# Reordering the start of a gated-MLP kernel: half-column products ahead of two turns, 16-bit turns, and one late product

## The chip, the cores and the metric

The kernel runs on one core of one Trainium2 chip. The metric is the device time of one execution in microseconds (us). Several executions are made of each kernel. "TensorE" is the matmul engine (PE in profile lines, PEld its weight loads), "VectorE" is DVE, "ScalarE" is ACT, "GpSimd" is POOL, "SyncE" is SP.

## The reference

```python
batch, seq, dim, hidden = 16, 256, 512, 2048
def reference(x, w1, w2):              # x (16,256,512), w1 (512,4096), w2 (2048,512), all float32
    h = x @ w1
    gate, value = np.split(h, 2, axis=-1)
    h = np.maximum(gate, 0) * value
    return (h @ w2).astype(np.float32)
```

## The kernel before

The 4096 rows of x are done in four groups of 1024, each as two halves of 512 rows. The hidden size is cut into 16 blocks of 128. Both matrix products use a seven-product scheme: instead of eight block products there are seven (P1 to P7), and some operands are sums. On the x side these are S1 to S4, made by VectorE in the first group; on the weight side T1 to T4, made by GpSimd:

```python
    def sums_of(o, eng=nc.vector):                       # S1 = A21+A22, S2 = S1-A11, S4 = A12-S2, S3 = A11-A21
        for n, i0, i1, op in (("S1", "A21", "A22", ADD), ("S2", "S1", "A11", SUB), ("S4", "A12", "S2", SUB),
                              ("S3", "A11", "A21", SUB)):
            yield eng.tensor_tensor(o[n], o[i0], o[i1], op=op)
# ... cut
    def w1_ops(jb, n, t):
        # ... cut
        nc.gpsimd.tensor_tensor(op["T1"], b12, b11, op=SUB)
        nc.gpsimd.tensor_tensor(op["T2"], b22, (op["T1"]), op=SUB)
        nc.gpsimd.tensor_tensor(op["T3"], b22, b12, op=SUB)
        nc.gpsimd.tensor_tensor(op["T4"], b21, (op["T2"]), op=SUB)
# ... cut
    WX = {"P1": ("B11", "A11"), "P2": ("B21", "A12"), "P3": ("B22", "S4"), "P4": ("T4", "A22"),
          "P5": ("T1", "S1"), "P6": ("T2", "S2"), "P7": ("T3", "S3")}
```

Block 2 is the first in this scheme. It needs S1 and T1 for P5, S2 and T2 for P6, S4 for P3, S3 and T3 for P7. Blocks 0 and 1 are "plain" (ordinary products), so that TensorE has work while the first sums and differences are made. The very first x rows come as float32 and are turned (transposed) by TensorE, four row blocks a half; each turn is evicted from PSUM by VectorE (one part) and then ScalarE (the other part). Fillers (`keep_busy`) are matmuls without a use.

```python
    def turn_first(o, h, b, ps):
        for e in range(4):
            nc.tensor.transpose(ps[:, e * P:(e + 1) * P], xn[h][b][:, e * P:(e + 1) * P], ident)
        for k, copy in ((0, nc.vector.tensor_copy), (1, nc.scalar.copy)):
            copy(out=o[f"A{h + 1}{k + 1}"][:, :, b * P:(b + 1) * P],
                 in_=ps[:, k * 256:k * 256 + 256].rearrange("p (b t) -> p b t", b=2))
# ... cut
    turn_first(xo, 0, 0, new_w())
    keep_busy(2)
    turn_first(xo, 0, 1, new_x())
    rest()
    keep_busy(4)
    turn_first(xo, 0, 2, new_x())
    keep_busy(2)
    turn_first(xo, 0, 3, new_w())
    keep_busy(2)
    plain[0].products(0, *first_half, half)
    # ... cut: weights of block 1, a fetch
    plain[0].products(0, *first_half, other)
    plain[0].value()                                     # ScalarE copies the value product
    plain[0].gate(0)                                     # VectorE: max(gate, 0) * value
    plain[1].products(0, *first_half, half)
    ps = [new_x(), new_w()]
    for b in range(4):
        turn_first(xo, 1, b, ps[b % 2])
        if b == 1:
            plain[1].products(0, *first_half, other)
            plain[1].value()
    plain[1].gate(0)
    sums = sums_of(xo)
    prepare(2)                                           # T1 to T4 of blocks 2 and 3
    copy_some(3)
    fetch(5, nc.sync)
    next(sums)                                           # S1
    plain[0].products(1, *second_half, half)
    next(sums)                                           # S2
    next(sums)                                           # S4
    plain[0].products(1, *second_half, other)
    plain[0].value()
    plain[0].gate(1)
    prepare(3)
    plain[1].products(1, *second_half)
```

In the lines of the profile, `x_A` is one of A11, A12, A22, and `x_S` one of S1 to S4 (A21 shares the place of S3), `w_T` one of T1 to T4.

## Time and profile before

| | before |
|---|---|
| device time, first measurement | 311.19 us median of 3 (311.07 to 311.42) |
| span of the profiled run | 309.2 us |
| TensorE busy | 301.5 us, 98% |
| TensorE idle after 23.73 us, until its last products | none shown |
| P4 of block 2 (the last stalled matmul) | 23.30 us |
| S1 on VectorE, T1 on GpSimd dispatched | 15.12 us, 15.57 us |

The page of the profile of the kernel before, part 1 (busy time, share of the span, number of instructions):

```profile
PE 301.5 (98%) x1870; PEld 183.2 (59%) x1870; DVE 236.4 (76%) x378; ACT 177.0 (57%) x350; POOL 153.7 (50%) x186
```

TensorE is the limit nearly everywhere. So a change at the start can win only by letting its unbroken run begin earlier. The timeline of the kernel before shows how that moment is set (columns: start in us, duration in us, engine, line, operation, output<-input, shapes, count, and in brackets the engine's idle time before it and what ended it):

```profile
15.12 0.68 DVE L164 TENSOR_TENSOR x_S<-x_S,x_A 128x1024 f16<-128x1024 f16 x1
15.57 1.36 POOL L215 TENSOR_TENSOR w_T<-w_stage 128x512 f16<-128x512 f32 x1 [5.44 <-DMA w_stage<-in_w_dram]
15.84 1.64 DVE L164 TENSOR_TENSOR x_S<-x_S,x_A 128x1024 f16<-128x1024 f16 x1
17.01 1.49 POOL L216 TENSOR_TENSOR w_T<-w_stage,w_T 128x512 f16<-128x512 f32 x1
17.51 1.53 DVE L164 TENSOR_TENSOR x_S<-x_A,x_S 128x1024 f16<-128x1024 f16 x1
18.45 1.72 POOL L217 TENSOR_TENSOR w_T<-w_stage 128x512 f16<-128x512 f32 x1
...
19.56 1.16 DVE L164 TENSOR_TENSOR x_S<-x_A,x_S 128x1024 f16<-128x1024 f16 x1
20.13 1.61 POOL L218 TENSOR_TENSOR w_T<-w_stage,w_T 128x512 f16<-128x512 f32 x1
...
23.30 0.59 PE L233 MATMUL Y<-x_A,w_T 128*128 128x512 f16 x2 [0.47 <-DVE cc L266]
```

The four VectorE lines are S1, S2, S4 and S3; the four GpSimd lines T1 to T4. All sums have the same shape, yet S1 takes 0.68 us and S2 1.64: S2 is dispatched at 15.84, when T1 is under way, and ends at 17.48, 0.55 us after T1's end (16.93), which is near the 0.68 us of an undisturbed sum. The Trainium skill (SBUF — State Buffer, "Who interferes with whom") says that a VectorE instruction with two SBUF inputs contends with a GpSimd instruction that reads SBUF, and that whoever issues first gets the shared ports for the whole instruction. The durations here fit that. From S1 to the `cc` that releases P4 at 23.30, VectorE has no recorded wait for another engine's result: its own instructions, held up by T1 to T4, set the moment.

The list of what TensorE waited for in the kernel before, from 5 us on (engine, what, line, waited for; total us, times, longest us):

```profile
PE X L448 <- DMA x_A<-in_x_dram: 0.8, 1, 0.8
PE Y L233 <- DVE cc L266: 0.5, 1, 0.5
PE X L233 <- ACT Y L240: 0.2, 1, 0.2
```

### The profile page before, as it was taken

To read this page: it belongs to the slowest core of one execution; us is meant where nothing else is said; L and a number is where in the kernel's file an instruction comes from. 1 tells how busy PE (TensorE), PEld (TensorE's weight loads), DVE (VectorE), ACT (ScalarE), POOL (GpSimd) and SP (SyncE) were. 2 spreads that over 40 slices of the span, in tenths; PEclk is the share of its full clock that TensorE was granted. 3 is DMA by queue.
4 is the path that set the end of the run, shared out by engine and by line. 5 is a ranking of instruction groups with operands and counts; after the bars stand their busy time and mean duration, and the time that the engine had idled before them with its cause. 6 is when DMAs were issued, how large, how long until landed. Compare 5 with 4: busy or idle time off the path is not lost.

```text
span 309.2 us, 5211 instructions
## 1 busy us (share of the span) xinstructions
PE 301.5 (98%) x1870; PEld 183.2 (59%) x1870; DVE 236.4 (76%) x378; ACT 177.0 (57%) x350; POOL 153.7 (50%) x186
## 2 busy tenths in 40 slices
PE   7999999999999999999999999999999999999994
PEld 3844444588854444478864444458884444448883
DVE  1598888889678888887538888888536888888841
ACT  2588886445865555537855555546956555553231
POOL 2199999930048899500028889700006988700000
PEclk9999999999999999999999999999999999999999
DMA  7977696998594233001354400000325110000132
GB/s 236 355 230 251 176 232 87 196 214 149 164 303 101 69 70 68 2 0 47 127 184 105 119 0 4 0 0 15 122 103 171 37 34 1 0 3 0 70 136 72
DMA packets 37340, 32.87 MB, mean 106 GB/s; under 512 B 14400, under 2 KB 32320, under 8 KB 37184
## 3 DMA queue, kind: packets, MB, share of 16 engines
q1 hardware_dynamic: 31904, 25.70, 27.2%
q0 software_dynamic: 4352, 6.29, 11.8%
q10 hardware_dynamic: 1056, 0.52, 0.6%
q8 instruction: 15, 0.25, 0.3%
q14 instruction: 13, 0.11, 0.1%
HBM read 27.26 MB, written 12.58 MB: 129 GB/s over the span
## 4 chain that ended last, share of the span: by engine, by line
PE 93%; DVE 2%; DMA 2%; issue 1%; SPq 0%; ACT 0%; DVEq 0%
PE Y L233 26%; PE X L233 17%; PE W L233 17%; PE Y L333 14%; PE X L333 9%; PE W L333 9%; DMA x_A<-in_x_dram 2%; DVE x_S L164 1%; PE X L448 1%; DVE g L308 1%; PE X L301 1%; PE W L301 1%; PE W L448 0%; PE Y L150 0%; DVE x_S L450 0%
## 5 line engine op out<-in xcount | busy, mean ns | idle before, releaser
L233 PEld LDWEIGHTS <-w_T 128*128 128x128 f16 x496 | 48.5, 98 | 57.5 <-issue 1.0
L170 POOL TENSOR_TENSOR fold<-xh 128x1024 f32<-128x1024 f16 x16 | 30.3, 1894 | 93.1 <-DMA xh<-x 92.1
L233 PE MATMUL X<-x_A,w_B 128*128 128x512 f16 x248 | 73.7, 379 | 0.2 <-ACT Y L240 0.2
L233 PE MATMUL Y<-x_S,w_T 128*128 128x512 f16 x248 | 73.8, 379 | 0.0
L233 PEld LDWEIGHTS <-w_B 128*128 128x128 f16 x372 | 36.4, 98 | 42.6 <-issue 0.8
L240 ACT COPY Y<-X 128x512 f32<-128x512 f32 x62 | 35.4, 570 | 39.8 <-PE X L233 39.5
L260 DVE SCALAR_TENSOR_TENSOR cc<-W,pu 128x512 f32<-128x512 f32 x62 | 42.8, 691 | 19.5 <-ACT pu L254 19.5
L254 ACT ACTIVATE pu<-Y 128x512 f32<-128x512 f32 x62 | 37.0, 597 | 34.1 <-PE Y L233 32.8
L173 POOL TENSOR_TENSOR fold<-fold 128x512 f32<-128x512 f32 (+2 forms) x96 | 51.8, 540 | 7.5
L333 PEld LDWEIGHTS <-w_stage 128*128 128x128 f16 x512 | 50.0, 98 | 6.3 <-issue 0.4
L266 DVE SCALAR_TENSOR_TENSOR cc<-Y,pu 128x512 f32<-128x512 f32 x62 | 42.8, 691 | 7.2 <-PE Y L233 0.7
L261 DVE SCALAR_TENSOR_TENSOR g<-X,cc 128x512 f16<-128x512 f32 x62 | 42.9, 691 | 2.3
L276 DVE SCALAR_TENSOR_TENSOR g<-Y,cc 128x512 f16<-128x512 f32 x62 | 42.2, 681 | 1.8 <-PE Y L233 1.8
L333 PEld LDWEIGHTS <-g 128*128 128x128 f16 x384 | 37.6, 98 | 8.2
L233 PE MATMUL Y<-x_A,w_T 128*128 128x512 f16 x124 | 36.9, 379 | 0.5 <-DVE cc L266 0.5
L247 ACT ACTIVATE pu<-W 128x512 f32<-128x512 f32 x62 | 37.2, 600 | 0.2 <-ACT Y L240 0.2
L233 PE MATMUL W<-x_S,w_T 128*128 128x512 f16 x124 | 36.9, 379 | 0.0
L233 PE MATMUL W<-x_S,w_B 128*128 128x512 f16 x124 | 36.9, 379 | 0.0
L333 PE MATMUL Y<-v_T,w_stage 128*128 128x256 f16 x256 | 33.2, 272 | 0.1
L333 PE MATMUL X<-v_B,g 128*128 128x256 f16 x256 | 31.9, 273 | 0.0
L164 DVE TENSOR_TENSOR w_stage<-g 128x1024 f16<-128x1024 f16 x32 | 21.5, 686 | 0.2
L365 DVE SCALAR_TENSOR_TENSOR o<-W,pu 128x256 f32<-128x256 f32 x16 | 6.7, 422 | 18.7 <-PE W L333 18.7
(84 smaller groups left out, 283.8 us busy)
## 6 DMA issues: line engine op xcount, KB each, us to landing
out_dram<-o SPq DMA_DIRECT2D x30, 256.0 KB, 2.0
w_stage<-in_w_dram SPq DMA_DIRECT2D x14, 512.0 KB, 5.7
x<-in_x_dram POOLq DMA_DIRECT2D x4, 1024.0 KB, 12.9
xh<-x SPq DMA_DIRECT2D x16, 256.0 KB, 3.1
v_B<-in_w_dram POOLq DMA_DIRECT2D x3, 512.0 KB, 6.3
x_S<-in_x_dram SPq DMA_DIRECT2D x4, 256.0 KB, 5.5
x_A<-in_x_dram SPq DMA_DIRECT2D x3, 256.0 KB, 4.9
w_stage<-in_w_dram ACTq DMA_DIRECT2D x2, 256.0 KB, 4.6
```

What stands on the lines that cost most here:

```text
L164: yield eng.tensor_tensor(o[n], o[i0], o[i1], op=op)
L170: nc.gpsimd.tensor_tensor(fold, t, t, op=MULT)
L173: nc.gpsimd.tensor_tensor(fold[:, :, :m], fold[:, :, :m], fold[:, :, m:2 * m], op=ADD)
L233: nc.tensor.matmul(ps, wop[wn][:, b, self.jb * P:(self.jb + 1) * P], self.xo[xn][:, b, :], start=fresh and b == 0, stop=b == 1, skip_group ...
L240: nc.scalar.copy(out=self.Y, in_=self.X)
L247: nc.scalar.activation(self.p5, self.W, COPY, scale=GS)
L254: nc.scalar.activation(self.u2, self.Y, COPY, scale=GS)
L260: nc.vector.scalar_tensor_tensor(out=self.c12, in0=self.W, scalar=GS, in1=self.u2, op0=MULT, op1=ADD)
L261: nc.vector.scalar_tensor_tensor(out=self.g[:, self.jb, :TH], in0=self.X, scalar=0.0, in1=self.c12, op0=MAX, op1=MULT)
L266: nc.vector.scalar_tensor_tensor(out=self.c22, in0=self.Y, scalar=GS, in1=self.p5, op0=MULT, op1=ADD)
L276: nc.vector.scalar_tensor_tensor(out=self.g[:, self.jb, TH:], in0=self.Y, scalar=0.0, in1=self.c22, op0=MAX, op1=MULT)
L333: nc.tensor.matmul(ps, self.op[an][:, i], vop[wn][:, i], start=name in ("P1", "P5") and i == 0, stop=i == NJ // 2 - 1, skip_group_check=True)
```

## The change

The intent was to take idle and useless time out of TensorE's start. (a) The products of block 0 on the first half of the columns run as soon as two turns are evicted, ahead of turns three and four; most fillers go. (b) The second half of the first x is cast to 16 bit before it is turned (two casts on VectorE, two on GpSimd), so that turns and evictions are shorter. (c) The last plain value product runs after P1 of block 2, to cover TensorE's 0.23 us wait for ScalarE's copy of P1. PSUM banks are handed out differently to allow it. The diff, cut:

```diff
-        def products(self, h, a1, a2, cols=(0, TH)):
+        def open(self, W=None): ...
+        def part(self, which, a1, a2, cols=(0, TH)): ...        # gate or value products alone
 # ... cut
+    x16_first = [halfs.tile(...) ... for _ in range(2)]
+    ident16 = wpool.tile([P, P], F16, name="ident16")
+    def cast_first(b, copy):
+        copy(out=x16_first[b // 2][:, b % 2], in_=xn[1][b])
-    def turn_first(o, h, b, ps):
+    def turn_first(o, h, b, *ps):
+        rows, one = (x16_first[b // 2][:, b % 2], ident16) if h else (xn[0][b], ident)
 # ... cut
-    turn_first(xo, 0, 0, new_w())
-    keep_busy(2)
-    turn_first(xo, 0, 1, new_x())
+    spare, turns2 = new_y(), new_y()
+    turn_first(xo, 0, 0, spare, turns2)
+    keep_busy(4)
+    turn_first(xo, 0, 1, new_x(), new_x())
     rest()
-    keep_busy(4)
-    turn_first(xo, 0, 2, new_x())
-    keep_busy(2)
-    turn_first(xo, 0, 3, new_w())
-    keep_busy(2)
-    plain[0].products(0, *first_half, half)
+    nc.tensor.matmul(spare, warm_b[:, :P], warm_b[:, :TH], start=True, stop=True)
+    plain[0].open()
+    plain[0].part("gate", *first_half, half)
+    plain[0].part("value", *first_half, half)
+    turns = new_x()
+    turn_first(xo, 0, 2, turns)
+    turn_first(xo, 0, 3, turns2)
 # ... cut
     plain[0].value()
+    cast_first(0, nc.vector.tensor_copy)
+    cast_first(1, nc.gpsimd.tensor_copy)
     plain[0].gate(0)
+    plain[1].open()
+    plain[1].part("gate", *first_half)
+    turns, turns2_16 = turns.bitcast(F16), turns2.bitcast(F16)
+    turn_first(xo, 1, 0, turns)
+    plain[1].part("value", *first_half, half)
+    turn_first(xo, 1, 1, turns2_16)
+    plain[1].part("value", *first_half, other)
+    plain[1].value()
+    cast_first(2, nc.gpsimd.tensor_copy)
+    cast_first(3, nc.vector.tensor_copy)
+    turn_first(xo, 1, 2, turns)
     plain[1].gate(0)
+    plain[0].open()
+    plain[0].part("gate", *second_half, half)
+    turn_first(xo, 1, 3, turns2_16)
 # ... cut: the rest of the plain products, the sums as before
+    def last_plain():                                    # called behind P1 of block 2
+        plain[1].part("value", *second_half)
+        plain[1].value()
+        next(sums)
+        plain[1].gate(1)
```

More of the change, by code (lines that the diff above doesn't have):

```diff
@@ L142, in fast_way @@
     ident = wpool.tile([P, P], F32, name="ident")
+    Y = psy.tile([P, TH], F32, name="Y", tag="Y")
     for i in range(NWARM):
-        Y = psy.tile([P, TH], F32, name="Y", tag="Y")
         nc.tensor.matmul(Y, warm_b[:, :P], warm_b[:, :TH], start=True, stop=True)
@@ L290, in __init__, with open, part @@
             self.g, self.jb = g, jb
-        def products(self, h, a1, a2, cols=(0, TH)):
+        def open(self, W=None):
+            self.X = psx.tile([P, TH], F32, name="X", tag="X")
+            self.W = psw.tile([P, TH], F32, name="W", tag="W") if W is None else W
+        def part(self, which, a1, a2, cols=(0, TH)):
             js, c = slice(self.jb * P, (self.jb + 1) * P), slice(*cols)
-            if cols[0] == 0:
-                self.X = psx.tile([P, TH], F32, name="X", tag="X")
-                self.W = psw.tile([P, TH], F32, name="W", tag="W")
-            for a, gate, value in ((a1, "B11", "T3"), (a2, "B21", "B22")):
-                for ps, wn in ((self.X, gate), (self.W, value)):
-                    for b in range(2):
-                        nc.tensor.matmul(ps[:, c], wop[wn][:, b, js], a[:, b, c], start=a is a1 and b == 0,
-                                         stop=a is a2 and b == 1)
+            ps, names = (self.X, ("B11", "B21")) if which == "gate" else (self.W, ("T3", "B22"))
+            for a, wn in zip((a1, a2), names):
+                for b in range(2):
+                    nc.tensor.matmul(ps[:, c], wop[wn][:, b, js], a[:, b, c], start=a is a1 and b == 0,
+                                     stop=a is a2 and b == 1)
         def value(self):
@@ L440, in fast_way @@
     xn = [[t.rearrange("p a b -> p (a b)").bitcast(F32) for t in place[4 * h:4 * h + 4]] for h in range(2)]
+    x16_first = [halfs.tile([P, 8, P], F16, name="xh", tag="xh").rearrange("p (b q) c -> p b (q c)", b=2) for _ in range(2)]
+    ident16 = wpool.tile([P, P], F16, name="ident16")
     def fetch_first(h):
@@ L444, in fetch_first, with new_y @@
             nc.sync.dma_start(out=xn[h][b], in_=x_nat[0, h, b])
-    def turn_first(o, h, b, ps):
+    def cast_first(b, copy):
+        copy(out=x16_first[b // 2][:, b % 2], in_=xn[1][b])
+    def turn_first(o, h, b, *ps):
+        rows, one = (x16_first[b // 2][:, b % 2], ident16) if h else (xn[0][b], ident)
+        if len(ps) == 1:
+            ps = ps[0][:, :2 * P], ps[0][:, 2 * P:]
         for e in range(4):
-            nc.tensor.transpose(ps[:, e * P:(e + 1) * P], xn[h][b][:, e * P:(e + 1) * P], ident)
+            nc.tensor.transpose(ps[e // 2][:, e % 2 * P:(e % 2 + 1) * P], rows[:, e * P:(e + 1) * P], one)
         for k, copy in ((0, nc.vector.tensor_copy), (1, nc.scalar.copy)):
             copy(out=o[f"A{h + 1}{k + 1}"][:, :, b * P:(b + 1) * P],
-                 in_=ps[:, k * 256:k * 256 + 256].rearrange("p (b t) -> p b t", b=2))
+                 in_=ps[k][:, :2 * P].rearrange("p (b t) -> p b t", b=2))
     def new_x():
         return psx.tile([P, TH], F32, name="X", tag="X")
-    def new_w():
-        return psw.tile([P, TH], F32, name="W", tag="W")
+    def new_y():
+        return psy.tile([P, TH], F32, name="Y", tag="Y")
     fetch(0, nc.scalar)
@@ L465, in fast_way @@
     fetch(3, nc.sync)
+    nc.vector.tensor_copy(out=ident16, in_=ident)
     xo = x_tiles()
@@ L470, in fast_way @@
     rest = plain_w(0)
-    turn_first(xo, 0, 0, new_w())
-    keep_busy(2)
-    turn_first(xo, 0, 1, new_x())
+    spare, turns2 = new_y(), new_y()
+    turn_first(xo, 0, 0, spare, turns2)
+    keep_busy(4)
+    turn_first(xo, 0, 1, new_x(), new_x())
     rest()
-    keep_busy(4)
-    turn_first(xo, 0, 2, new_x())
-    keep_busy(2)
-    turn_first(xo, 0, 3, new_w())
-    keep_busy(2)
-    plain[0].products(0, *first_half, half)
+    nc.tensor.matmul(spare, warm_b[:, :P], warm_b[:, :TH], start=True, stop=True)
[5 more added lines that the diff above has]
+    turn_first(xo, 0, 3, turns2)
     plain_w(1)()
     fetch(4, nc.sync)
-    plain[0].products(0, *first_half, other)
+    plain[0].part("gate", *first_half, other)
+    plain[0].part("value", *first_half, other)
     plain[0].value()
+    cast_first(0, nc.vector.tensor_copy)
+    cast_first(1, nc.gpsimd.tensor_copy)
     plain[0].gate(0)
-    plain[1].products(0, *first_half, half)
-    ps = [new_x(), new_w()]
-    for b in range(4):
-        turn_first(xo, 1, b, ps[b % 2])
-        if b == 1:
-            plain[1].products(0, *first_half, other)
-            plain[1].value()
-    plain[1].gate(0)
+    plain[1].open()
[9 more added lines that the diff above has]
+    turn_first(xo, 1, 2, turns)
+    plain[1].gate(0)
+    plain[0].open()
+    plain[0].part("gate", *second_half, half)
+    turn_first(xo, 1, 3, turns2_16)
+    plain[0].part("value", *second_half, half)
+    plain[1].open(turns2)
+    plain[1].part("gate", *second_half, half)
     sums = sums_of(xo)
@@ L498, in fast_way @@
     next(sums)
-    plain[0].products(1, *second_half, half)
     next(sums)
+    plain[0].part("gate", *second_half, other)
+    plain[0].part("value", *second_half, other)
+    plain[0].value()
     next(sums)
-    plain[0].products(1, *second_half, other)
-    plain[0].value()
     plain[0].gate(1)
     prepare(3)
-    plain[1].products(1, *second_half)
+    plain[1].part("gate", *second_half, other)
+    def last_plain():
[3 more added lines that the diff above has]
+        plain[1].gate(1)
     LOOKX, looks = {}, []
@@ L595, in fast_way @@
                 if s == 0 and (n, jb) == ("P1", NPLAIN):
-                    plain[1].value()
-                if s == 0 and (n, jb) == ("P5", NPLAIN):
-                    next(sums)
-                    plain[1].gate(1)
+                    last_plain()
                 if n in ("P6", "P7"):
```

## The prediction

> **What bounds it now.** The list of busy times has TensorE at 98% of 309.2 us, and the chain of waits is 93% TensorE. The timeline of TensorE shows no idle time from 23.73 us to the end, so the change can only move the moment at which that unbroken run begins. Before it, TensorE waits 0.78 us for x rows (6.24 us), 0.23 for ScalarE's Y copy (18.64) and 0.47 for VectorE's `cc` of block 2 (23.30), and runs eight filler matmuls after 6.24 us (0.11 us each, 0.87 us).
>
> **Removed.** The eight fillers become one 512-column filler (0.22 us): 0.65 us less TensorE. The four later turns take 0.43 us each as 32 bit. The Trainium skill (TensorE: Matmul & The Clock Gate, Back-to-back issue gap) gives about 81 ns for a 128-column pair; no run here shows it yet. I estimate 0.32 us a turn, 0.4 less in all. Moving the last value product (0.86 us) behind P1 of block 2 hides the 0.23 us wait. At most 1.3 us of TensorE time.
>
> **Added.** Four casts of 128x512 (two on VectorE, about 0.4 us each; two on GpSimd, about 0.7 us each, from its 0.40 us for 256 elements). New waits: turns three and four now follow the half-column products, so their evictions (VectorE 0.42, then ScalarE 0.37, one after the other on a bank) end at about 9.95 us, not 9.49, and TensorE waits about 0.9 us for them. The first block's first half ends at 10.64 us (10.42 before).
>
> **What decides.** VectorE runs without a gap from 15.12 us (the first sum S1) to the end of the `cc` that releases TensorE at 23.30. There the sums alternate with GpSimd's T1 to T4: S1 alone takes 0.68 us, S2 takes 1.64, S4 1.53, S3 1.16; S2 ends after T1 ends. The Trainium skill (SBUF — State Buffer, Who interferes with whom) says that a VectorE instruction with two SBUF inputs and a GpSimd one that reads SBUF exclude each other for the whole instruction; those durations agree. T1 starts at 15.57 us, when its weights land: transfers run at about 350 GB/s from 3 us, unchanged. So what counts is when S1 starts, and that is after the last turn's ScalarE eviction.
>
> After the change: value copy of block 0 ends 11.44; gate to 12.15; evictions of turns (second half) 1 and 2 to 13.4 on ScalarE; value copy of block 1 to 14.0; gate to 14.7; last eviction 14.95 on VectorE, 15.3 on ScalarE. S1 then starts at about 15.35, 0.2 us later than before but ahead of T1. With 16-bit evictions still at 0.42 us it would come near 15.6, behind T1, and every sum would fall behind one T: about 2 us lost. If it starts by 14.8, S1 and S2 both pass ahead of T1, and about 0.75 us is won. T4 (ends at 21.74) allows at most 1.5 us.
>
> **Prediction.** Most of TensorE's gain turns into waits: 311.0 us, 8 times in 10 between 309.9 and 312.4. Faster by over 2%: 0.01; within 2%: 0.97; slower by over 2%: 0.02.
>
> **What would show it.** Later turns at 0.25 to 0.35 us; their VectorE evictions at 0.29; TensorE idle before the products after turn four; start of S1 between 14.8 and 15.5, T1 still at about 15.5; P4 of block 2 still released by VectorE's `cc`, between 22.5 and 23.7 us (23.30 before); no idle TensorE afterwards, so the times differ by that matmul's shift.
>
> **What would make it wrong.** S1 behind T1 (about 313). Or S1 early enough that T4 or TensorE sets P4 (about 310). Or later weights limiting a TensorE that runs ahead.

## The result and the profile after

| | before | after |
|---|---|---|
| device time, median (4 runs each) | 311.31 us (311.07 to 311.74) | 311.86 us (311.23 to 312.18) |
| ratio | | 1.0014, 95% interval 0.9994 to 1.0034 |
| span of the profiled run | 309.2 us | 310.4 us |
| S1, T1 dispatched | 15.12, 15.57 us | 15.42, 15.34 us |
| P4 of block 2 | 23.30 us | 24.54 us |
| last group of eight matmuls (one line of the timeline) starts | 303.50 us | 304.75 us |

A ratio is the mean time of one kernel's runs over that of the other's of the same rounds, so it is not quite the ratio of the medians quoted. By the ratio the two kernels are the same; the profiled run of the changed kernel was its slowest, and its P4 is 1.24 us late. From P4 of block 2 to the last group TensorE takes 280.20 us before (303.50 minus 23.30) and 280.21 after: the whole difference of these two profiled runs lies before P4.

Page of the changed kernel, part 1:

```profile
PE 302.0 (97%) x1865; PEld 182.5 (59%) x1865; DVE 238.2 (77%) x381; ACT 176.7 (57%) x350; POOL 155.3 (50%) x188
```

Timeline of the changed kernel, the lines that answer to those of before:

```profile
14.10 0.69 DVE L310 SCALAR_TENSOR_TENSOR g<-X,v 128x512 f16<-128x512 f32 x1 [0.21 <-ACT v L307]
14.71 0.28 DVE L462 COPY x_S<-Y 128x256 f16<-128x256 f16 x1
15.02 0.37 ACT L462 COPY x_A<-Y 128x256 f16<-128x256 f16 x1 [0.69 <-DVE x_S L462]
15.34 1.28 POOL L215 TENSOR_TENSOR w_T<-w_stage 128x512 f16<-128x512 f32 x1 [3.16 <-DMA w_stage<-in_w_dram]
15.42 1.74 DVE L164 TENSOR_TENSOR x_S<-x_S,x_A 128x1024 f16<-128x1024 f16 x1 [0.44 <-ACT x_A L462]
...
17.20 1.53 DVE L164 TENSOR_TENSOR x_S<-x_S,x_A 128x1024 f16<-128x1024 f16 x1
...
18.76 1.64 DVE L164 TENSOR_TENSOR x_S<-x_A,x_S 128x1024 f16<-128x1024 f16 x1
...
20.46 0.60 PE L233 MATMUL W<-x_S,w_B 128*128 128x512 f16 x2 [1.09 <-DVE x_S L164]
...
24.54 0.59 PE L233 MATMUL Y<-x_A,w_T 128*128 128x512 f16 x2 [0.54 <-DVE cc L266]
```

Now T1 is dispatched first, by 0.08 us. S1 takes 1.74 us instead of 0.68, and every later sum falls behind one more T. P3 of block 2 needs S4 and waits 1.09 us for it (the line at 20.46); P4 follows at 24.54. The lines above S1 show why S1 is late: the gate of block 1 (14.10) stands ahead of the last eviction on VectorE (14.71), ScalarE's part of that eviction comes behind it (15.02), and S1 waits for that.

The chain of waits of the changed kernel, from the eviction of turn four on (start, us, what; 12.87 is the eviction of the second half's second turn). Left out are TensorE's pieces from 9.87 to 12.61 us and the pieces called `issue`, of 0.05 us at most:

```profile
9.39 0.44 DVE x_A L462
12.61 0.24 PE Y L460 x4
12.87 0.30 DVE x_S L462
13.19 0.37 ACT x_A L462
13.56 0.51 ACT v L307
14.10 0.69 DVE g L310
14.79 0.21 DVE x_S L462
15.02 0.38 ACT x_A L462
15.42 1.75 DVE x_S L164
```

From 12.87 us it goes through VectorE and ScalarE alone. Ahead of that, from 9.87 to 12.85, it is TensorE's work one after the other, behind the eviction of turn four and so behind the wait for it. TensorE's new order thus helps to set the moment of S1; what it saves counts only as far as it moves that moment. The list of TensorE's waits in the changed kernel, from 5 us on:

```profile
PE W L233 <- DVE x_S L164: 1.1, 1, 1.1
PE X L302 <- DVE x_A L462: 0.6, 1, 0.6
PE Y L233 <- DVE cc L266: 0.5, 1, 0.5
```

The wait for ScalarE's Y copy (0.2) went, as intended. The wait for x rows (0.8) went from the list only because four fillers now stand in it: turn two starts at 6.23 us, against 6.24 before. A wait of 0.6 us for the evictions of turns three and four and one of 1.1 us for S4 came.

### The profile page after: what moved, and what is told of

Read it like the earlier page. It is cut to its first block, busy times and chain, and to the rows that moved or that the text cites. A ratio compares the mean times of both kernels' runs of the same rounds, so it can differ in the third digit from the quotient of the medians.

```text
span 310.4 us, 5203 instructions
## 1 busy us (share of the span) xinstructions
PE 302.0 (97%) x1865; PEld 182.5 (59%) x1865; DVE 238.2 (77%) x381; ACT 176.7 (57%) x350; POOL 155.3 (50%) x188
## 4 chain that ended last, share of the span: by engine, by line
PE 94%; DVE 4%; ACT 1%; issue 1%; DVEq 0%
PE Y L233 25%; PE X L233 17%; PE W L233 17%; PE Y L335 14%; PE X L335 9%; PE W L335 9%; DVE x_S L164 2%; PE Y L145 1%; PE X L302 1%; DVE g L310 1%; PE Y L460 0%; PE W L302 0%; DVE x_A L462 0%; PE X L460 0%; PE Y L150 0%
```

## The experiments

Two theories were put against each other. **Port order:** the time is set by whether S1 or T1 is dispatched first, and so by when S1's inputs are ready. **TensorE order:** the time is set by what TensorE does in the new order, chiefly its wait after turn four. They do not exclude each other in full, since the chain above shows TensorE's order among the things that set S1's moment; what the runs can decide is whether that order counts apart from S1's moment. All twelve runs had five rounds beside the kernel before; that kernel's own runs in these groups spread from 310.9 to 312.8 us (one at 314.3, in the group of the last four runs of the table, where it lowers all four ratios), so differences of a few tenths are read from the profiles, at P4 of block 2, more safely than from the medians. The table collects all of them (us):

| run | S1 | T1 | P4, block 2 | last group | median | ratio to before (95%) |
|---|---|---|---|---|---|---|
| before | 15.12 | 15.57 | 23.30 | 303.50 | 311.31 | |
| after | 15.42 | 15.34 | 24.54 | 304.75 | 311.86 | 1.0014 (0.9994 to 1.0034) |
| a_again | 15.25 | 15.43 | 23.44 | 304.08 | 312.07 | 1.0012 (0.9993 to 1.0030) |
| gate_late | 15.04 | 15.50 | 23.24 | 303.57 | 311.61 | 1.0000 (0.9981 to 1.0019) |
| b_delay | 15.52 | 15.51 | 24.70 | 304.92 | 312.42 | 1.0021 (1.0001 to 1.0041) |
| t_write (wrong result) | 15.25 | none | 22.08 | 302.30 | 310.01 | 0.9954 (0.9935 to 0.9972) |
| b_16 | 14.17 | 15.34 | 22.02 | 302.96 | 310.89 | 0.9988 (0.9975 to 1.0001) |
| b_last | 14.93 | 15.38 | 23.12 | 303.58 | 311.37 | 1.0001 (0.9988 to 1.0014) |
| half_only | 16.33 | 15.50 | 24.69 | 304.90 | 312.60 | 1.0041 (1.0028 to 1.0054) |
| best (wrong result) | 14.26 | 15.40 | 22.05 | 303.09 | 311.06 | 0.9989 (0.9977 to 1.0002) |
| b_16_cast | 14.30 | 15.46 | 22.16 | 302.51 | 310.51 | 0.9968 (0.9935 to 1.0002) |
| b_16_last_cast | 14.32 | 15.49 | 22.06 | 303.17 | 311.02 | 0.9987 (0.9953 to 1.0021) |
| best2 | 14.35 | 15.55 | 22.15 | 303.62 | 310.99 | 0.9977 (0.9945 to 1.0009) |
| b_cast | 14.95 | 15.38 | 23.12 | 303.33 | 311.26 | 0.9987 (0.9952 to 1.0021) |

### a_again: the changed kernel once more

No edit. Expected:

> The changed kernel itself, again. Port-order theory (VectorE's first sum S1 and GpSimd's first weight difference T1 of block 2 race for the shared SBUF port; whichever starts first holds it): the runs spread over 0.5 us or more, from about 311.2 (S1 first) to about 312.3 (T1 first); a profile with S1 at over 1.5 us has P3 of block 2 waiting about 1.1 us for S4 and P4 at about 24.5 us, one with S1 at 0.68 us has no such wait and P4 at about 23.5. TensorE-order rival (the 0.59 us wait after turn four and what follows on TensorE set the time): runs agree within 0.3 us, whatever S1 takes.

The five runs took 311.79 to 312.34 us, so the medians agree with the first measurement. The spread of 0.55 us is what was expected, but it decides nothing: the eleven runs of the kernel before in the same group spread over 1.93 us. In the profile of this run (a timeline, like those above) S1 is first:

```profile
15.25 0.69 DVE L164 TENSOR_TENSOR x_S<-x_S,x_A 128x1024 f16<-128x1024 f16 x1 [0.44 <-ACT x_A L462]
15.43 1.64 POOL L215 TENSOR_TENSOR w_T<-w_stage 128x512 f16<-128x512 f32 x1 [3.17 <-DMA w_stage<-in_w_dram]
...
23.44 0.59 PE L233 MATMUL Y<-x_A,w_T 128*128 128x512 f16 x2 [0.54 <-DVE cc L266]
...
85.90 0.60 PE L335 MATMUL Y<-v_T,g 128*128 128x256 f16 x4 [0.26 <-DVE o L372]
```

The same program: S1 takes 0.69 us and T1 1.64 (it is now T1 that waits), and P4 comes at 23.44 us, 1.10 us earlier than in the first profile. So the order at the port is not fixed in the changed kernel, and it is worth 1.1 us there. S1's 0.17 us come from far ahead: the eviction of turn three is already 0.18 us earlier (8.70 against 8.88 us). But my expectation that such a run takes 311.2 us failed: this one took 312.07. It lost 0.42 us later, and the last line shows where: a wait near 86 us that the first two profiles don't have (the brackets show 0.26 us of it, the rest is hidden in the modelled end of the matmul before). That second limit comes up again below.

### gate_late: the gate of block 1 behind S1

```diff
     turn_first(xo, 1, 2, turns)
-    plain[1].gate(0)
+    early = Plain(g, 1)
+    early.X, early.v = plain[1].X, plain[1].v
 # ... cut
     next(sums)
+    early.gate(0)
     next(sums)
```

> The changed kernel with the gate of block 1's first half moved on VectorE from before the last turn's eviction to behind S1. Port-order theory: S1 starts at about 14.95 us instead of 15.42, takes 0.68 us, T1 waits for it; the 1.1 us wait of P3 of block 2 is gone, P4 at 23.2 to 23.5 us, 311.0 +- 0.3 us, and the runs agree within 0.4 us. TensorE-order rival: TensorE's work and order are the same and its wait after turn four too, so 311.9 +- 0.3.

S1 came at 15.04, 0.46 us ahead of T1, and P3's wait was gone; P4 came at 23.24, as the port-order theory said. TensorE's wait of 0.59 us after turn four was still there, so that wait, though it lies ahead of S1, does not by itself lose the race. The median of 311.61 us misses the expected 311.0 +- 0.3 and the runs spread over 0.91 us (311.11 to 312.02), more than expected: the median alone does not tell the theories apart, the profile does.

### b_delay: S1 held back in the kernel before

```diff
+    nc.vector.tensor_copy(out=late, in_=ps[1][:, :late.shape[1]])    # 128x384 from PSUM
     sums = sums_of(xo)
     prepare(2)
```

> The kernel before with one VectorE copy of 128x384 from PSUM (about 0.5 us) put ahead of S1; nothing else touched. Port-order theory: S1 is then dispatched at about 15.65 us, behind T1 at 15.57, takes about 1.6 us, P3 of block 2 waits 0.6 us or more for S4, and the kernel loses 1.0 to 1.6 us (312.2 to 312.8): more than the 0.5 us that the copy takes. TensorE-order rival, or a plain VectorE chain without the port: it loses 0 to 0.5 us.

Timeline of b_delay:

```profile
15.06 0.55 DVE L495 CAST late<-W 128x384 f16<-128x384 f32 x1
...
15.51 1.28 POOL L216 TENSOR_TENSOR w_T<-w_stage 128x512 f16<-128x512 f32 x1 [5.44 <-DMA w_stage<-in_w_dram]
15.52 1.80 DVE L165 TENSOR_TENSOR x_S<-x_S,x_A 128x1024 f16<-128x1024 f16 x1
...
20.62 0.61 PE L234 MATMUL W<-x_S,w_B 128*128 128x512 f16 x2 [1.02 <-DVE x_S L165]
...
24.70 0.59 PE L234 MATMUL Y<-x_A,w_T 128*128 128x512 f16 x2 [0.54 <-DVE cc L267]
```

A copy of 0.55 us, with nothing of the change in it, makes the picture of the changed kernel: S1 takes 1.80 us, P3 waits 1.02 us for S4, P4 is 1.40 us late. The loss is more than twice the copy. In the times it is 1.0021, with an interval that just excludes no change.

### t_write: T1 to T4 that read nothing

For blocks 2 and 3 only, GpSimd waits for the same weights (two one-column copies) and then fills T1 to T4 with ones.

```diff
+        if jb == 2:
+            nc.gpsimd.tensor_copy(out=late[:, :1], in_=b12[:, 0, :1])
+            nc.gpsimd.tensor_copy(out=late[:, :1], in_=b22[:, 0, :1])
+            for name in ("T1", "T2", "T3", "T4"):
+                nc.gpsimd.memset(op[name], 1.0)
+        else: ...                                        # T1 to T4 as before
```

> The changed kernel with T1 to T4 of blocks 2 and 3 replaced by GpSimd memsets that start when the same weights have landed (wrong result on purpose: these weights are 1). Port-order theory: a memset reads no SBUF, so S1, S2, S4 and S3 take 0.68 us each, P3 and P4 of block 2 wait for nothing much, P4 starts at about 22.3 us and the kernel takes about 310.0 us. TensorE-order rival: S1 may shorten, but the time stays above 311.3. If T1 to T4's own durations were the limit (not the port), the sums would still take over 1 us each here.

VectorE's timeline in t_write, the four sums:

```profile
15.25 1.42 DVE L165 TENSOR_TENSOR x_S<-x_S,x_A 128x1024 f16<-128x1024 f16 x2 [0.44 <-ACT x_A L469]
16.70 0.69 DVE L165 TENSOR_TENSOR x_S<-x_A,x_S 128x1024 f16<-128x1024 f16 x1
...
17.91 0.68 DVE L165 TENSOR_TENSOR x_S<-x_A,x_S 128x1024 f16<-128x1024 f16 x1
```

The four memsets (1.92 us together, from 16.65 us) lie over S4, which takes 0.69 us all the same. So it is not GpSimd's being busy that stretches a sum, but its reading SBUF. P4 came at 22.08 us without a wait and the kernel took 310.01 us, as expected to the tenth. This run also has T2 to T4 ready earlier, so its P4 is not a measure of the port alone; the durations of the sums are.

### b_16, b_last, half_only: the three parts, each alone

b_16 puts the casts and 16-bit turns into the kernel before, in the old order (third and fourth casts ahead of turn three, on GpSimd and VectorE):

```diff
+    cast_first(0, nc.vector.tensor_copy)
+    cast_first(1, nc.gpsimd.tensor_copy)
     plain[0].gate(0)
     plain[1].products(0, *first_half, half)
-    ps = [new_x(), new_w()]
+    ps = [new_x().bitcast(F16), new_w().bitcast(F16)]
```

> The kernel before with the 16-bit turns of the second half alone (casts as in the change; order of products and turns, and the last value product, as before). Port-order theory: the first block's value copy stays at about 10.6 us, the later evictions are shorter, so S1 starts at about 14.4 us and S1 and S2 are both done or under way before T1; P4 of block 2 at about 22.3 us instead of 23.30, and the kernel is 0.7 to 1.2 us faster than before (310.2 to 310.6). Rival (16-bit turns bring the loss, by their casts and the waits on them): slower than before, S1 after 15.1.

VectorE's timeline in b_16, S1 and S2 in one line, then S4:

```profile
14.17 1.41 DVE L164 TENSOR_TENSOR x_S<-x_S,x_A 128x1024 f16<-128x1024 f16 x2
15.61 1.64 DVE L164 TENSOR_TENSOR x_S<-x_A,x_S 128x1024 f16<-128x1024 f16 x1
```

S1 and S2 take 1.41 us together, both ahead of T1 (15.34), and P4 comes at 22.02 us, 1.28 us earlier than before, without a wait for VectorE; its chain of waits is TensorE's own work but for one ScalarE copy (0.58 us) from 11.54 us on. The 16-bit turns are the helpful part. But the median is only 310.89 us: 0.4 us below its neighbours of before (311.30), and the interval just reaches 1. The lead was 1.27 us at 63 us and 0.54 us at 93 us; it was given back between, with a wait of 0.28 us near 85 us like the one in a_again.

b_last moves the last value product alone:

```diff
-    plain[1].products(1, *second_half)
+    plain[1].products(1, *second_half, only="gate")
+    def last_plain():                                    # called behind P1 of block 2
+        plain[1].products(1, *second_half, only="value")
+        plain[1].value()
+        next(sums)
+        plain[1].gate(1)
```

> The kernel before with the last plain value product moved behind P1 of block 2 alone. Port-order theory: the 0.23 us wait for ScalarE's Y copy goes, S1 and T1 stay at 15.1 and 15.5, P4 of block 2 is still set by VectorE at 23.2 to 23.4 us: no change of the time (within 0.2 us). Rival (TensorE's own time counts): 0.2 us or more faster.

The wait for the Y copy went; P4 stayed with VectorE. It came at 23.12 us, but S1 and T1 were 0.19 us early in this run as well (14.93 and 15.38), which is all of the 0.18. Time unchanged (1.0001), but that is no clean test: TensorE lost about 0.26 us near 85 us in this profile (a start-to-start of 0.70 us where 0.43 is usual), so the 0.18 us would not have shown. P4 shows it better: where VectorE sets P4, the wait ahead of it cost nothing.

half_only has the half-column products ahead of turns three and four, with the changed PSUM banks, but float32 turns and the last product in its old place:

```diff
-        rows, one = (x16_first[b // 2][:, b % 2], ident16) if h else (xn[0][b], ident)
+        rows, one = xn[h][b], ident
 # ... cut: no casts; plain[1].part("value", *second_half) and its value and gate in the old places
```

> The changed kernel without the 16-bit turns and with the last value product in its old place: the half-column products ahead of turns three and four alone (with the PSUM buffers that come with it). Port-order theory: the first value copy comes 0.5 us late as in the changed kernel, the later turns are no shorter, S1 starts at 15.6 us or later, behind T1; P4 of block 2 at 24.5 us or later; 1.0 to 1.6 us slower than before (312.2 to 312.8). Rival (the half-column move is the helpful part, the harm is in the 16-bit turns): not slower than before.

S1's inputs were ready at 16.33 us, behind T1 at 15.50. P4 came at 24.69 us, and this was the only kernel whose loss is clear of noise by a good margin: 1.0041 (1.0028 to 1.0054), all five runs between 312.49 and 312.91 us. The new order is the harmful part. The run does not split it further: the half-column products, the banks and the new places of the turns and the gate came together. Its chain of waits runs through TensorE from the wait after turn four to the third turn of the second half (14.35 us), and on through VectorE and ScalarE to S1: here TensorE's new order does set S1's moment.

### best: the evictions ahead of the gate

Here the changed kernel's last two turns go earlier and into other PSUM banks, the fourth cast goes to GpSimd, ScalarE's value copy and VectorE's gate of block 1 go behind the evictions, and the gate behind S2.

```diff
     turn_first(xo, 1, 1, turns2_16)
+    cast_first(2, nc.gpsimd.tensor_copy)
+    cast_first(3, nc.gpsimd.tensor_copy)
+    turn_first(xo, 1, 2, spare.bitcast(F16))
     plain[1].part("value", *first_half, other)
+    turn_first(xo, 1, 3, new_y().bitcast(F16))
     plain[1].value()
 # ... cut: the old places of the casts and turns, and the gate behind S2
```

> The changed kernel with all evictions of the second half ahead of block 1's value copy and gate, the fourth cast on GpSimd, the last two turns in free PSUM banks and earlier on TensorE, and the gate behind S2. Port-order theory: S1 at about 14.3 us, S2 at about 15.0, both ahead of T1 and 0.7 us each; P4 of block 2 at about 22.1 to 22.5 us; about 310.2 us, 1 us faster than before. Rival: if TensorE's earlier waits decided, these are as in the changed kernel (0.59 us after turn four), so 311.5 or more.

The result was wrong (relative error 0.21), which was not intended. A 16-bit turn fills the first 1 KB of a bank, as a matmul that starts its own sum; later block 2's Y is put into such a bank by ScalarE and added to by matmuls without a start flag. The Trainium skill (PSUM — Partial Sum Buffer, "The four PSUM rules") says that a start flag clears the accumulate bits of the whole 2 KB bank, and that a matmul without it overwrites where the bit is clear. That fits: with the turns moved to banks that a full-width matmul with a start flag fills first (best2 below), the result is right. The work and the waits are those of a right kernel, so its profile is used: S1 at 14.26, S1 and S2 in 1.42 us together, P4 at 22.05 us as expected, with TensorE's 0.59 us wait after turn four still there. The median, 311.06 us, missed the expected 310.2, by a give-back of the same kind as in b_16: its lead fell from 1.23 us at 63 us to 0.41 at 93 us.

### b_16_cast, b_16_last_cast, best2, b_cast: the second limit

In b_16, VectorE's timeline near 83 us has this line, the first two sums of the next x group:

```profile
82.65 1.42 DVE L164 TENSOR_TENSOR x_S<-x_S,x_A 128x1024 f16<-128x1024 f16 x2 [2.98 <-DMA x_A<-x]
```

VectorE waits 2.98 us there for the turned loads of the next x, and evictions of the second product queue behind it. The theory was that the three casts of x, issued together by GpSimd, slow one another down. All four runs move the cast of the third group:

```diff
-    CASTS = {(0, 11): 1, (0, 13): 0, (0, 14): 2, (1, 8): 3}
+    CASTS = {(0, 11): 1, (0, 13): 0, (0, 15): 2, (1, 8): 3}
```

b_16_cast is b_16 with it, b_16_last_cast has the last product too, best2 is the mended best, b_cast is the kernel before.

> The 16-bit turns alone on the kernel before, and the cast of the third x group moved on GpSimd from block 14 of the first group to block 15, behind the two long weight differences of the second product. Theory of the second limit (the gain of 1.27 us is given back to 0.54 between 75 and 90 us because VectorE waits there for the next x group's turned loads, whose cast shares the transfer engines with the other two casts): the next x lands 1 us or more earlier (before 81.7 us instead of 82.65), the 0.28 us wait of TensorE near 85 us is gone, the lead of P4 of block 2 (22.0 us) is kept to the end, span 307.9 to 308.1 and about 309.8 us. Rival (the late loss is VectorE's own work): unchanged at 310.9.

> The same with the last plain value product behind P1 of block 2 too. Now that VectorE no longer sets P4, TensorE's 0.23 us wait for the Y copy is on the path: P4 of block 2 at 21.7 to 21.9 us (GpSimd's T4 ends at about 21.1), about 309.6 us. Rival: T2 or the sums hold it at 22.0, same as without.

> The reordered changed kernel again, mended (the last two 16-bit turns go to banks that a matmul with a start flag fills before they are added to, so the result is right), with the cast moved as well: S1 at 14.3 us, P4 of block 2 at 22.0 us as in the wrong one, the lead kept past 85 us, about 309.9 us.

> The kernel before with only the cast moved: a control. TensorE there does not wait near 85 us, so no change: 311.2 +- 0.3 us, P4 of block 2 at 23.2 to 23.4 us; the next x lands earlier (before 82 us) all the same.

The cast theory fell. The casts did get shorter (median from issue to landing 11.3 us in b_16_cast, 14.6 in b_16), but the first sum of the next x came at 82.20, 82.85, 83.30 and 82.88 us in the four runs, not before 81.7 or 82. Only b_16_cast kept most of its lead (1.14 us at 63 us, 0.99 at 93); b_16_last_cast fell from 1.24 to 0.34 and best2 from 1.15 to 0.11 behind before. Taking the last product into b_16 moved P4 from 22.16 to 22.06, less than the 21.7 to 21.9 expected. b_cast shows no change of the time, as a control should.

TensorE's longest late wait in best2, from its timeline:

```profile
85.44 0.60 PE L335 MATMUL Y<-v_T,g 128*128 128x256 f16 x4 [0.80 <-DVE o L372]
```

One relation holds over all runs that waited there. Add 220.3 us to the moment at which VectorE's first sum of the next x starts, and the last group's start comes out: 82.65 gives 302.95 (b_16, measured 302.96), 82.20 gives 302.50 (302.51), 82.85 gives 303.15 (303.17), 83.30 gives 303.60 (303.62), 82.78 gives 303.08 (best, 303.09), 83.76 gives 304.06 (a_again, 304.08). Two more runs lie on it, with losses too short for the list of waits: 83.25 gives 303.55 (gate_late, 303.57), 83.28 gives 303.58 (b_last, 303.58). The constant is fitted to these runs. So the landing of the next x is a second floor. It varied from 82.20 to 83.76 us in these runs, hardly following the lead (82.20 to 83.30 in the five kernels that lead by over 1 us), and it caps what an earlier start can win. In the kernel before it is close already: 83.03 us there gives 303.33, only 0.17 us under the measured 303.50. So without an earlier landing hardly any of a lead at P4 could have been kept. In t_write it was no floor: there GpSimd issued the casts about 3 us earlier (51.4 us against 54.5), and VectorE's sum started at 80.86 without a recorded wait for a load. That makes an earlier issue of the casts the obvious next thing to try; no run tried it alone. What those loads wait for between their first issue at 64 us and 82 us stays open.

## Why the prediction was right, and where it was not

The measured 311.86 us lies in the range of 309.9 to 312.4, and "within 2%" was right, which says little: the median of every kernel run here, the failed ones too, lies within 0.5% of the kernel before. That the range held is partly luck: the first profile is of a run that lost to T1, which the prediction put at about 313, outside its range, and only because losing cost less than the 2 us assumed did it stay inside. Point by point:

- **The path.** That only the start of TensorE's unbroken run counts, that VectorE's chain from S1 to `cc` sets it, and that S1's moment against T1's decides, was right: a_again, gate_late and b_delay show it. That the start alone counts was not always so: a_again, b_16, b_last, best, b_16_last_cast and best2 lost time again near 85 us.
- **S1's moment.** Predicted 15.35 us; measured 15.42 and 15.25. The steps to it fit as well: 16-bit evictions on VectorE 0.28 us (0.29 predicted), the gate of block 1 ended at 14.79 (14.7), the last ScalarE eviction to 15.39 and 15.21 (15.3).
- **T1's moment, the term that was mis-sized.** The prediction took T1 as fixed at the 15.57 us of the one profile of before and concluded that S1 is "ahead of T1". In the 12 other profiles with a T1 it came at 15.34 to 15.55 us. With S1 at 15.25 to 15.42 that is a tie, not a lead of 0.2 us. The case "S1 behind T1", which the prediction named as what would make it wrong, is the one in the first profile.
- **The size of losing.** Predicted about 2 us; measured 1.24 us (after), 1.40 (b_delay) and 1.39 (half_only) against P4 of before; in the same program, lost against won, 1.10.
- **The central value.** 311.0 us is 0.2 below the time before, though the prediction's own sum put S1 0.2 us later with S1 ahead. That sum was right for a_again (P4 0.14 us later than before). The lower value had no step behind it.
- **TensorE's terms.** A 16-bit turn takes 0.22 to 0.24 us in the chain of waits, below the predicted 0.32. The wait after turn four was 0.59 us, not 0.9, and the first block came later (its value copy ended at 11.72 us, not 11.44). These terms are on the chain that leads to S1 (from 9.39 to 12.87 us), where they nearly cancel: the value copy is 0.28 us later than predicted, S1 only 0.07.

Why the change wins nothing is thus shown in parts: the 16-bit turns bring S1 forward (b_16: 14.17 us), the new order around the half-column products puts it back (half_only: 16.33 us), together they leave it in a tie with T1 (15.42 and 15.25), and the last product does not move P4 while VectorE sets it (b_last). How often the changed kernel loses the tie was seen in two profiles only (once lost, once won), so its mean cost is not known. And with x landing as in the profile of before, any lead of over 0.17 us would have met the floor near 85 us.

No version with a right result is shown to be better than the kernel before. b_16_cast has the lowest right median, 310.51 us against 311.44 of its group; the ratio is 0.9968, and its interval reaches 1.0002. The run at 314.3 us of the kernel before is in that group; without it the ratio of the means is 0.9973, so a gain of some 0.3% is likely and not shown.

## What to carry to other kernels

When two engines exclude each other at a shared port, the order of dispatch can be worth more than the length of an instruction (here 1.10 us against 0.68): look for equal instructions with unequal durations, and give the one on the path a margin larger than the scatter of the other's start. Time taken out of the busiest engine in a start-up phase is worth nothing until the chain that releases its last stall is known; here its last part ran over evictions and a gate on other engines. And before moving a start forward, look for the next event that does not move with it, here a load landing at 82 to 84 us.

## What the Trainium skill lacked or had wrong

- TensorE: Matmul & The Clock Gate, "Back-to-back issue gap": it gives about 81 ns for a load-and-multiply pair with 128 columns in a stream. The changed kernel's four 16-bit turns of 128 columns took 0.22 to 0.24 us each from start to start, 55 to 60 ns a pair. The prediction's 0.32 us a turn came from the 81.
- SBUF — State Buffer, "Who interferes with whom": its rule was confirmed in both directions (S1 1.74 us behind T1; T1 1.64 us behind S1) and for memsets (S4 0.69 us beside them). It does not say what happens when both engines go on with such instructions: here they alternated, each sum behind one difference (S2 1.64, S4 1.53, S3 1.16 us). Losing the first turn at the port put the whole row of sums back once: P4 came 1.10 us later in the same program (24.54 against 23.44), about one blocked instruction's 1.06 (1.74 minus 0.68).
- PSUM — Partial Sum Buffer, "The four PSUM rules": nothing was missing that best's wrong result (relative error 0.21) needed. The notes under its second rule also say that a transpose of 2-byte elements clears the bits of its bank whatever its flag, which I had overlooked.
